# RWKV projections: both heads' keys written by two 128-partition VectorE operations, the second head's kinds change places in the store's DMAs

## The chip, the cores and the metric

The kernel runs on one core of one Trainium2 chip. The metric is the device time of one execution in microseconds (us), the median over several runs. Engine names are those of the profile: PE is the matrix engine, PEld its weight loads, DVE is VectorE, ACT is ScalarE, POOL is GpSimd and SP is SyncE, which issues almost every DMA of this kernel. A name with a q (SPq, DVEq) is an engine's instruction queue: DMA issues and waits.

## The reference

One block of a diffusion backbone, 512 latent tokens and 256 context tokens of width 1024, in two layers: the first mixes tokens with a bidirectional RWKV-7 recurrence, the second with a Hyena long convolution, each between two half-step SwiGLU layers. Only the RWKV mixer's preparation matters here. For each of 16 heads of 64 channels, two directions d and all 768 tokens it needs:

```
k   = xk @ w_k;  r = xr @ w_r;  v = xv @ w_v
a   = sigmoid(a0[d] + lora_a(xa)[d]);  decay = exp(-exp(-softplus(-w_pre[d]) - 0.5))
kk  = normalized(k * k_k)
kd  = k * (1 + (a - 1) * k_a)        # key of the direction
ka  = kk * a                         # removal key
S_t = S_{t-1} (diag(w_t) - kk_t ka_t^T) + v_t kd_t^T;   y_t = S_t r_t
```

The recurrence is computed in chunks of 64 tokens, so keys and queries are scaled with cumulated decays (`Ep`, `Em`) before they are used. The two scaled keys of a chunk, `ka * EK` and `kd * EK`, are the two kinds that this case is about.

## The kernel before, in words

All arithmetic is in f32; the large products split each operand in a high and a low part and take three matmuls (lines 471 to 473). Channels lie on the 128 partitions, tokens along the free dimension. A tile of 128 channels holds two heads: head 0 on partitions 0 to 63, head 1 on 64 to 127.

`rwkv_proj` (line 688) computes the projections one after the other: k, then r (line 901), v (line 910) and the gate's 160 columns (line 933). While r, v and the gate are projected, it draws steps out of `rwkv_prep` (line 943) with `ahead` (line 894), so that the preparation of the recurrence runs beside the matmuls. The order within an engine is worked out at compile time, by a scheduler that simulates the program; it takes what is issued first as the more urgent.

`rwkv_prep` works on 16 items: 8 tiles of 128 channels, each in two halves of 384 tokens (6 chunks of 64). Each item goes through three generators that run one pass apart: `front` loads k and r back from scratch memory (lines 975, 976), computes `kk` (line 982) from a small product on PE (line 980) and the low-rank products (lines 993, 994, 996, 997); `middle` makes the scaled keys and queries for both directions; `back` sums a bonus term (lines 1059 to 1066).

In `middle`, for each direction: line 1016 writes `ka` (one buffer), line 1019 is the scan over the decays, lines 1023 and 1024 are the two exponentials on ACT (`Ep` has one buffer), line 1021 writes `kd`, lines 1033 and 1034 write the tile `AR`, line 1036 the product `rb`. Lines 1039 to 1043 write the tile `KD`, of shape 128 x 6 chunks x 2 kinds x 64 tokens, with two buffers: head 0 holds (ka, kd) in the places 0 and 1, head 1 holds them the other way round, (kd, ka). So each of the two heads takes one operation for `ka` (line 1042) and one for `kd` (line 1043), 64 partitions each. Line 1042 is on POOL for the first 14 items and on DVE for the last two (line 1012, `NVEC` is 2); line 1043 is always on DVE. Then two DMAs on SP's queue store `AR` (line 1047) and `KD` (line 1050) into the scratch tensors `S_A` and `S_K`; a store of `KD` writes runs of 512 bytes, both kinds of one chunk side by side.

POOL has other work in the same stretch: line 1036 for the first 14 items, low parts of weights and of mixed tokens (line 477), low parts of the low-rank weights (line 963) and small memsets.

After the preparation `rwkv_scan` (line 1084) reads `S_A` and `S_K`: lines 1130 and 1134 load both kinds of two chunks, line 1198 is its first product, line 1152 loads one chunk of keys. They rely on the swapped places of head 1.

Stores whose shape bears on the change stand in line 926: they write v from 64 partitions in 6 runs of 256 bytes each, 96 KB in all.

Of the kernel before, what the change touches and what calls it, by code (L numbers as in the profile page):

```python
# [13 lines left out]
ALU = mybir.AluOpType  # L14
# [259 lines left out]
class K:  # L274
# [668 lines left out]
    def rwkv_prep(self, bp):  # L943
        nc = self.nc
        cE = 0.5 * math.exp(-0.5)
        W = TA // 2
        nch = W // 64
        c3 = lambda ap: ap.rearrange("p (c t) -> p c t", t=64)
        l2 = {}

        def ps(w):
            return self.psq.tile([P, 512], F32, tag="pq", name=self.nm("pq"))[:, :w]

        def T(tag, w=W, bufs=2):
            return bp.tile([P, W], F32, tag=tag, name=self.nm(tag), bufs=bufs)[:, :w]

        def lora2(m):
            raw = bp.tile([P, 4, P], F32, tag="l2r", name=self.nm("l2r"), bufs=1)
            hi = bp.tile([P, 4, P], F32R, tag="l2h", name=self.nm("l2h"), bufs=1)
            lo = bp.tile([P, 4, P], F32R, tag="l2l", name=self.nm("l2l"), bufs=1)  # L960
            nc.sync.dma_start(raw, self.A["wa2"][m])
            nc.scalar.copy(hi, raw)
            nc.gpsimd.tensor_tensor(lo, raw, hi.bitcast(F32), ALU.subtract)
            l2[m] = (hi, lo)

        lora2(0)

        def front(s):
            m, half = s["m"], s["half"]
            mc = slice(m, m + 1)  # L970
            o = s["o"] = half * W
            wl = s["wl"] = min(TL - o, W)
            s["nl"] = wl // 64
            k, r = T("k"), T("r", wl)
            nc.sync.dma_start(k, self.S_k[m][:, o : o + W])
            nc.sync.dma_start(r, self.S_r[m][:, o : o + wl])
            hi, lo = l2[m]
            yield
            pb = ps(W)
            nc.tensor.matmul(pb, self.selT[:, m * P : (m + 1) * P], self.kinv[:, o : o + W], start=True, stop=True)  # L980
            kk = s["kk"] = T("kk")
            nc.vector.scalar_tensor_tensor(kk, k, self.hkk[:, mc], pb, ALU.mult, ALU.mult)
            s["k"], s["r"] = k, r
            yield
            s["q"], s["a"] = [], []
            for d in range(2):
                q = bp.tile([P, nch, 65], F32, tag=f"q{d}", name=self.nm("q"))
                a = T(f"a{d}")
                nc.gpsimd.memset(q[:, :, 0:1], 0.0)
                rows = slice(d * 64, d * 64 + 64)  # L990
                for j, (x, t) in enumerate(((self.midw, q[:, :, 1:]), (self.mida, a))):
                    pt = ps(W)
                    nc.tensor.matmul(pt, hi[:, 2 * j + d], x[d][:, o : o + W], start=True, stop=False)
                    nc.tensor.matmul(pt, lo[rows, 2 * j + d], x[d][rows, o : o + W], start=False, stop=True)
                    b = (self.hw0, self.ha0)[j][:, d, mc]
                    nc.scalar.activation(t, c3(pt) if j == 0 else pt, AF.Tanh, bias=b, scale=0.5)
                nc.vector.tensor_scalar(q[:, :, 1:], q[:, :, 1:], 1.0, None, ALU.add)
                s["q"].append(q)
                s["a"].append(a)
                if d == 1 and half == 0 and m < DT - 1:  # L1000
                    lora2(m + 1)
                yield

        def middle(s):
            m, half, wl, nl = s["m"], s["half"], s["wl"], s["nl"]
            g, p_ = divmod(m, NP)
            c0 = s["o"] // 64
            mc = slice(m, m + 1)
            k, r, kk = s["k"], s["r"], s["kk"]
            s["b"] = []  # L1010

            pool = nc.vector if s["i"] >= 16 - NVEC else nc.gpsimd
            for d in range(2):
                q, a = s["q"][d], s["a"][d]
                ka, kd = T("ka", W, 1), a
                nc.vector.scalar_tensor_tensor(ka, a, 1.0, kk, ALU.add, ALU.mult)
                nc.scalar.activation(a, a, AF.Identity, bias=self.omka[:, mc], scale=self.hka[:, mc])
                qf = q.rearrange("p c t -> p (c t)")
                nc.vector.tensor_tensor_scan(qf, self.c("scan"), qf, 0.0, ALU.mult, ALU.add)
                yield  # L1020
                nc.vector.tensor_mul(kd, k, a)
                Ep = bp.tile([P, nch, 65], F32, tag="Ep", name=self.nm("Ep"), bufs=1)
                nc.scalar.activation(Ep, q, AF.Exp, scale=cE)
                nc.scalar.activation(q, q, AF.Exp, scale=-cE)
                Em = q
                nc.scalar.copy(self.PC[:, m, d, c0 : c0 + nch].unsqueeze(2), Em[:, :, 64:65])
                yield
                if d == 0:
                    EA, ER, EK = Em[:, :, 0:64], Em[:, :nl, 1:65], Ep[:, :, 1:65]
                else:  # L1030
                    EA, ER, EK = Ep[:, :, 1:65], Ep[:, :nl, 0:64], Em[:, :, 0:64]
                AR = bp.tile([P, nch, 2, 64], F32, tag="AR", name=self.nm("AR"), bufs=2)
                nc.vector.scalar_tensor_tensor(AR[:, :, 0], c3(kk), 2.0, EA, ALU.mult, ALU.mult)
                nc.vector.tensor_mul(AR[:, :nl, 1], c3(r), ER)
                rb = T("rb", wl, 1) if d == 0 else r
                pool.tensor_tensor(rb, r, kd[:, :wl], ALU.mult)
                s["b"].append(rb)
                yield
                KD = bp.tile([P, nch, 2, 64], F32, tag="KD", name=self.nm("KD"), bufs=2)
                for hh in range(2):  # L1040
                    h_ = slice(hh * 64, hh * 64 + 64)
                    pool.tensor_tensor(KD[h_, :, hh], c3(ka)[h_], EK[h_], ALU.mult)
                    nc.vector.tensor_mul(KD[h_, :, 1 - hh], c3(kd)[h_], EK[h_])
                if nl < nch:
                    nc.gpsimd.memset(AR[:, nl:, 1], 0.0)
                x = (g, d, half)
                nc.sync.dma_start(
                    self.S_A[x][:, :, p_].rearrange("c p s t -> p c (s t)"), AR.rearrange("p c s t -> p c (s t)")
                )
                nc.sync.dma_start(  # L1050
                    self.S_K[x][:, :, p_].rearrange("c p s t -> p c (s t)"), KD.rearrange("p c s t -> p c (s t)")
                )
                yield

        def back(s):
            m, wl, o = s["m"], s["wl"], s["o"]
            pt = ps(wl)
            rks = bp.tile([P, P], F32, tag="rks", name=self.nm("rks"), bufs=1)
            nc.scalar.activation(rks, self.c("bo64"), AF.Copy, scale=self.rk32[:, m : m + 1])
            yield  # L1060
            for d in range(2):
                nc.tensor.matmul(pt, rks, s["b"][d], start=d == 0, stop=d == 1)
            yield
            v = s["b"][0]
            nc.scalar.copy(v, pt)
            nc.sync.dma_start(self.S_b[s["m"]][:, o : o + wl], v)
            yield

        items = [dict(i=2 * m + 1 - half, m=m, half=half) for m in range(DT) for half in (1, 0)]
        n = len(items)  # L1070
        for i in range(n + 2):
            gens = []
            if 0 <= i - 2:
                gens.append(back(items[i - 2]))
            if 0 <= i - 1 < n:
                gens.append(middle(items[i - 1]))
            if i < n:
                gens.append(front(items[i]))
            while gens:
                gens = [x for x in gens if next(x, 0) is None]  # L1080
                yield
# [1031 lines left out]
```

## Time and profile before

| | us |
|---|---|
| median of 3 runs (lowest to highest) | 3119.48 (3110.41 to 3122.94) |
| the profiled execution's own time | 3117.68 |
| its span, first to last instruction | 3116.0 |
| PE busy in the span | 2848.1 (91%) |
| DVE busy | 1859.3 (60%) |
| ACT busy | 1202.1 (39%) |
| POOL busy | 504.5 (16%) |

The busy shares are averages over the whole kernel; the stretch in which `rwkv_prep` runs, from about 790 to 1050 us, looks otherwise. A row of a view of groups of instructions reads: line, engine, operation, tile written <- tiles read, shape, count, then busy us and mean ns of one, then the idle time of the engine just before them and what ended it. A row of windows reads: stretch, its length, busy us of each engine with the number of instructions, then the granted share of the TensorE clock, the mean busy share of the 16 DMA engines and the GB/s they moved.

### The profile page before, as it was taken

The page shows a single profiled execution, that of the slowest core. Times are in us where ns is not written, and L with a number is a line of the kernel's source. Part 1 is how long each engine was busy: PE and PEld are TensorE (multiplying, and loading weights), DVE is VectorE, ACT ScalarE, POOL GpSimd, SP SyncE. Part 2 cuts the span into 40 slices and gives each one's busy share as a digit, 9 for nine tenths or more (in the row PEclk, how much of TensorE's full clock was granted, in tenths as well). Part 3 has the DMA queues.
Part 4 walks back from the last instruction along what each step waited for, and adds up shares of the span by engine and source line. Part 5 has one row for each costly group of instructions (what it writes and reads, how often), then busy time and mean ns, then how long its engine had stood idle before and what let it go on. Part 6 is the DMA issues. An engine that isn't in the chain of part 4 may idle for free.

```text
span 3116.0 us, 46929 instructions
## 1 busy us (share of the span) xinstructions
PE 2848.1 (91%) x18698; PEld 2378.4 (76%) x18698; DVE 1859.3 (60%) x3261; ACT 1202.1 (39%) x2003; POOL 504.5 (16%) x571
## 2 busy tenths in 40 slices
PE   8999999978989567888799999999999988899998
PEld 4888888856656356776688889888896777888888
DVE  5744543473899778888754454554446578653334
ACT  3221121364555678885332222422234322242222
POOL 0000000032566344552100000000000044200000
PEclk9999999988979668898899999999999999999999
DMA  6533531313566643433634464344342454333221
GB/s 233 170 108 102 163 104 65 98 41 103 170 180 182 176 123 111 129 109 90 192 119 149 135 202 136 103 168 142 115 144 91 169 179 166 112 99 105 95 97 53
DMA packets 350084, 407.29 MB, mean 131 GB/s; under 512 B 52055, under 2 KB 289751, under 8 KB 348136
## 3 DMA queue, kind: packets, MB, share of 16 engines
q1 hardware_dynamic: 349864, 404.29, 40.9%
q8 instruction: 147, 2.41, 0.3%
q14 instruction: 73, 0.60, 0.1%
HBM read 338.10 MB, written 65.34 MB: 129 GB/s over the span
## 4 chain that ended last, share of the span: by engine, by line
PE 49%; DVE 7%; ACT 5%; DMA 2%; issue 2%; POOL 1%; SPq 0%; DVEq 0%; POOLq 0%; ACTq 0%
PE ps L471 14%; PE ps L472 14%; PE ps L473 14%; PE sc L1198 1%; ACT XT L1288 1%; ACT AG L1174 1%; DVE Dl L1265 1%; DVE wlo L477 1%; DVE Tm L1258 1%; PE pf L1747 1%; ACT Dl L1223 1%; DVE zl L477 1%; DVE SV L1337 1%; DVE zt L1934 1%; PE ps L414 0%
## 5 line engine op out<-in xcount | busy, mean ns | idle before, releaser
L471 PE MATMUL ps<-hh,whi 128*128 128x512 f32 (+1 forms) x2064 | 733.3, 363 | 14.3 <-ACT hh L264 11.0
L472 PE MATMUL ps<-hl,whi 128*128 128x512 f32 (+1 forms) x2064 | 742.6, 362 | 3.0 <-DVE hl L265 3.0
L473 PE MATMUL ps<-hh,wlo 128*128 128x512 f32 (+1 forms) x2064 | 736.5, 362 | 1.6 <-DVE wlo L477 1.6
L477 DVE TENSOR_TENSOR wlo<-raw,whi 128x1024 fp32r<-128x1024 f32 (+1 forms) x325 | 392.4, 1213 | 407.0 <-ACT whi L476 402.9
L476 ACT CAST whi<-raw 128x1024 fp32r<-128x1024 f32 (+1 forms) x338 | 344.5, 1028 | 720.0 <-PE ps L472 648.7
L471 PEld LDWEIGHTS ps<-hh,whi 128*128 128x128 f32 x2064 | 386.6, 190 | 79.7 <-ACT hh L264 13.3
L472 PEld LDWEIGHTS ps<-hl,whi 128*128 128x128 f32 x2064 | 393.0, 190 | 62.8 <-DVE hl L265 4.0
L473 PEld LDWEIGHTS ps<-hh,wlo 128*128 128x128 f32 x2064 | 391.9, 190 | 64.2 <-DVE wlo L477 2.3
L472 PE MATMUL ps<-dl,whi 128*128 128x512 f32 (+1 forms) x1072 | 358.1, 335 | 0.0
L473 PE MATMUL ps<-dh,wlo 128*128 128x512 f32 (+1 forms) x1072 | 357.8, 335 | 0.0
L471 PE MATMUL ps<-dh,whi 128*128 128x512 f32 (+1 forms) x1072 | 356.8, 337 | 0.0
L601 DVE TENSOR_TENSOR sg<-sg,ps 128x512 f32<-128x512 f32 (+1 forms) x110 | 69.1, 632 | 259.1 <-PE ps L473 249.7
L472 PEld LDWEIGHTS ps<-dl,whi 128*128 128x128 f32 x1072 | 204.2, 191 | 20.4
L471 PEld LDWEIGHTS ps<-dh,whi 128*128 128x128 f32 x1072 | 203.8, 191 | 20.9
L473 PEld LDWEIGHTS ps<-dh,wlo 128*128 128x128 f32 x1072 | 203.9, 190 | 20.6
L408 DVE SCALAR_TENSOR_TENSOR macc<-mraw,cs,macc 128x1024 f32<-128x1024 f32 x133 | 168.7, 1282 | 81.7 <-DMA mraw<-in_mod_w 80.5
L1779 POOL TENSOR_SCALAR G<-G 128x512 f32<-128x512 f32 x8 | 11.9, 1492 | 937.3 <-ACT G L1770 919.9
L600 ACT ACTIVATE sg<-ps 128x512 f32<-128x512 f32 (+1 forms) x110 | 59.6, 552 | 229.8 <-PE ps L473 216.9
L476 ACT CAST dh<-sg 128x512 fp32r<-128x512 f32 (+1 forms) x110 | 62.4, 575 | 214.0 <-DVE sg L601 213.8
L472 PE MATMUL ps<-xl,whi 128*128 128x512 f32 (+2 forms) x336 | 131.3, 392 | 11.0 <-DVE xl L798 6.3
L471 PE MATMUL ps<-xh,whi 128*128 128x512 f32 (+2 forms) x336 | 128.3, 395 | 10.2 <-ACT xh L805 6.5
L647 DVE SCALAR_TENSOR_TENSOR x<-ps,der,x 128x512 f32<-128x512 f32 (+1 forms) x128 | 82.5, 663 | 84.4 <-PE ps L473 84.3
(315 smaller groups left out, 4759.5 us busy)
## 6 DMA issues: line engine op xcount, KB each, us to landing
raw<-in_wgu SPq DMA_DIRECT2D x88, 1024.0 KB, 5.0
mraw<-in_mod_w SPq DMA_DIRECT2D x144, 512.0 KB, 4.3
raw<-in_wd SPq DMA_DIRECT2D x24, 1024.0 KB, 4.8
raw<-in_wrkv SPq DMA_DIRECT2D x12, 1024.0 KB, 5.2
S_A<-AR SPq DMA_DIRECT2D x32, 384.0 KB, 3.2
S_K<-KD SPq DMA_DIRECT2D x32, 384.0 KB, 3.3
AG<-S_A SPq DMA_DIRECT2D x48, 256.0 KB, 4.2
KK<-S_K SPq DMA_DIRECT2D x24, 512.0 KB, 4.5
```

What stands on the lines that cost most here:

```text
L408: nc.vector.scalar_tensor_tensor(acc, raw, sc, acc, ALU.mult, ALU.add)
L471: nc.tensor.matmul(out, wh, xh, start=start, stop=False)
L472: nc.tensor.matmul(out, wh, xl, start=False, stop=False)
L473: nc.tensor.matmul(out, wl, xh, start=False, stop=stop)
L476: self.nc.scalar.copy(hi, src)
L477: (self.nc.gpsimd if pool else self.nc.vector).tensor_tensor(lo, src, hi.bitcast(F32), ALU.subtract)
L600: nc.scalar.activation(sg, pg, AF.Silu)
L601: nc.vector.tensor_mul(sg, sg, pu)
L647: nc.vector.scalar_tensor_tensor(X[m][:, o : o + w], pt, gates[who][:, m : m + 1], X[m][:, o : o + w], ALU.mult, ALU.add)
L1174: nc.scalar.copy(dst, src)
L1198: nc.tensor.matmul(sc[:, p_, :, :ns, :], KK[:, c, p_].rearrange("p s t -> p (s t)"), AG[:, c, :, p_, :ns, :], start=True, stop=True,)
L1223: nc.scalar.copy(BD[r].rearrange("p t c -> p c t"), Bcc[r, :, b : b + 32])
```

## The change

The two kinds of both heads are written to the same places, so that one operation of 128 partitions writes `ka` for both heads and one writes `kd`; both are on DVE, for all 16 items. The places of head 1 are swapped in the store: where one DMA stored `KD`, three do, one for head 0 (64 partitions, runs of 512 bytes) and one for each kind of head 1 (64 partitions, runs of 256 bytes, 96 KB each). What lies in `S_K` is the same as before.

```
                 KD = bp.tile([P, nch, 2, 64], F32, tag="KD", name=self.nm("KD"), bufs=2)
-                for hh in range(2):
-                    h_ = slice(hh * 64, hh * 64 + 64)
-                    pool.tensor_tensor(KD[h_, :, hh], c3(ka)[h_], EK[h_], ALU.mult)
-                    nc.vector.tensor_mul(KD[h_, :, 1 - hh], c3(kd)[h_], EK[h_])
+                nc.vector.tensor_mul(KD[:, :, 0], c3(ka), EK)
+                nc.vector.tensor_mul(KD[:, :, 1], c3(kd), EK)
                 if nl < nch:
                     nc.gpsimd.memset(AR[:, nl:, 1], 0.0)
                 x = (g, d, half)
                 nc.sync.dma_start(
                     self.S_A[x][:, :, p_].rearrange("c p s t -> p c (s t)"), AR.rearrange("p c s t -> p c (s t)")
                 )
-                nc.sync.dma_start(
-                    self.S_K[x][:, :, p_].rearrange("c p s t -> p c (s t)"), KD.rearrange("p c s t -> p c (s t)")
-                )
+
+                sk = self.S_K[x][:, :, p_].rearrange("c p s t -> p c s t")
+                nc.sync.dma_start(sk[:64].rearrange("p c s t -> p c (s t)"), KD[:64].rearrange("p c s t -> p c (s t)"))
+                for j in range(2):
+                    nc.sync.dma_start(sk[64:, :, 1 - j], KD[64:, :, j])
                 yield
```

## Rows read from the trace of the kernel before

**Rows 1.** Windows: busy us of each engine, granted clock, DMA share, GB/s.

```profile
790.00:820.00 30.00, 30.00 (x121) 21.45 (x121) 28.27 (x35) 20.22 (x39) 16.48 (x18) 1.00 0.66 195
790.00:1022.00 232.00, 200.03 (x785) 139.74 (x785) 221.32 (x274) 136.31 (x281) 145.70 (x146) 0.85 0.65 184
1022.00:1050.00 28.00, 15.29 (x45) 7.38 (x43) 26.88 (x49) 16.76 (x32) 5.64 (x6) 0.74 0.57 158
```

**Rows 2.** Groups of instructions by shape, DVE, 790 to 1022 us.

```profile
L1019 DVE TENSOR_TENSOR_SCAN q<-cst,q 128x390 f32<-128x390 f32 x29 | 39.6, 1366 | 0.9
L1021 DVE TENSOR_TENSOR a<-k,a 128x384 f32<-128x384 f32 x28 | 26.1, 931 | 1.8 <-ACT a L1017 1.8
L1043 DVE TENSOR_TENSOR KD<-a,q 64x384 f32<-64x384 f32 x28 | 25.1, 898 | 0.7
L1016 DVE SCALAR_TENSOR_TENSOR ka<-a,kk 128x384 f32<-128x384 f32 x29 | 25.0, 864 | 1.6 <-ACT a L996 1.3
L1043 DVE TENSOR_TENSOR KD<-a,Ep 64x384 f32<-64x384 f32 x28 | 23.7, 847 | 1.6 <-ACT Ep L1023 1.3
L997 DVE TENSOR_SCALAR q<-q 128x384 f32<-128x384 f32 x29 | 16.2, 559 | 1.4 <-ACT q L996 1.0
L1033 DVE SCALAR_TENSOR_TENSOR AR<-kk,q 128x384 f32<-128x384 f32 x14 | 11.6, 827 | 2.5 <-ACT q L1024 2.3
L1033 DVE SCALAR_TENSOR_TENSOR AR<-kk,Ep 128x384 f32<-128x384 f32 x14 | 10.4, 741 | 0.1
```

**Rows 3.** The same view, DVE, 1026 to 1050 us, where POOL is nearly idle.

```profile
L1019 DVE TENSOR_TENSOR_SCAN q<-cst,q 128x390 f32<-128x390 f32 x3 | 2.9, 963 | 0.0
...
L1043 DVE TENSOR_TENSOR KD<-a,Ep 64x384 f32<-64x384 f32 x4 | 2.2, 550 | 0.0
...
L1033 DVE SCALAR_TENSOR_TENSOR AR<-kk,Ep 128x384 f32<-128x384 f32 x2 | 1.1, 550 | 0.0
...
L997 DVE TENSOR_SCALAR q<-q 128x384 f32<-128x384 f32 x2 | 0.7, 343 | 0.0
```

**Rows 4.** The same view, POOL, 790 to 1022 us.

```profile
L1042 POOL TENSOR_TENSOR KD<-ka,q 64x384 f32<-64x384 f32 x28 | 34.1, 1219 | 23.2 <-ACT q L1024 16.1 <-DVE ka L1016 4.5 <-DVE AR L1034 1.5
L1042 POOL TENSOR_TENSOR KD<-ka,Ep 64x384 f32<-64x384 f32 x28 | 33.1, 1183 | 16.7 <-ACT Ep L1023 11.4 <-ACT PC L1026 3.1 <-issue 0.6
```

**Rows 5.** Waits of PE, 790 to 1022 us: total us, times, longest.

```profile
PE ps L919 <- ACT ev L828: 7.3, 6, 3.8
PE ps L471 <- ACT xh L476: 3.7, 2, 2.7
```

**Rows 6.** Timeline of DVE, last item: start us, us, line, operation.

```profile
1047.65 0.54 DVE L1042 TENSOR_TENSOR KD<-ka,q 64x384 f32<-64x384 f32 x1
1048.12 0.54 DVE L1043 TENSOR_TENSOR KD<-a,q 64x384 f32<-64x384 f32 x1
1048.68 0.56 DVE L1042 TENSOR_TENSOR KD<-ka,q 64x384 f32<-64x384 f32 x1
1049.16 0.55 DVE L1043 TENSOR_TENSOR KD<-a,q 64x384 f32<-64x384 f32 x1
1049.74 0.56 DVE L1036 TENSOR_TENSOR r<-r,a 128x384 f32<-128x384 f32 x1
```

**Rows 7.** Lines 1050 and 926: issue of a store, ns min/median/max, first and last start.

```profile
L1050 SPq DMA_DIRECT2D S_K<-KD x32: 359/371/2082, 799.0 to 1049.7; - x32
...
L926 SPq DMA_DIRECT2D S_V<-vt x32: 587/632/2837, 892.5 to 1015.1; - x32
```

**Rows 8.** DMA issues, 790 to 1050 us: count, KB each, median us to landing.

```profile
S_K<-KD SPq DMA_DIRECT2D x32, 384.0 KB, 3.3
...
S_V<-vt SPq DMA_DIRECT2D x32, 96.0 KB, 2.5
```

**Rows 9.** Timeline of SP and PE where the scan begins.

```profile
1046.17 0.54 SPq L1050 DMA_DIRECT2D S_K<-KD  x1
1046.76 0.62 SPq L1134 DMA_DIRECT2D KK<-S_K  x1
...
1050.99 3.76 PE L1198 MATMUL ps<-AG,KK 128*128 128x128 f32 x16 [4.86 <-issue]
```

## The prediction

> **What bounds the kernel now.** I read the page first: PE is 91% busy over the span, DVE 60%, POOL 16%. These averages say nothing about the place that the change touches, so the windows over the stretch of the preparation come next [rows 1]. From 790 to 1022 us DVE is busy 221.3 of 232 us, 95%, and in the tail to 1050 us 26.9 of 28, 96%. PE is busy 200.0 of the 232 us, at a mean granted clock of 0.85 of its upper level, 2.4 GHz. So DVE sets the pace here, and PE, whose matmuls stand in order between the preparation's small products, waits for what DVE makes. Only in the first 30 us is PE full, at clock 1.00.
>
> The second reading is what DVE's busy time is made of: the same operation compared in two stretches. From 1026 us on POOL has almost nothing left, and a DVE operation on 384 elements with two inputs takes 550 ns, the scan 963, line 997 343 [rows 3]. Before 1022 us, with POOL at work, the same shapes take 741 to 931, 1366 and 559 ns [rows 2]. The extra time is no work; it is what a neighbour costs. Over the eight groups of rows 2 it is 28 x 381 + 28 x 348 + 28 x 297 + 29 x 314 + 14 x 277 + 14 x 191 for the operations of 384 elements, 29 x 403 for the scan and 29 x 216 for line 997: 62.4 us.
>
> **What the change removes.** First, 56 operations of line 1042 leave POOL, 34.1 + 33.1 = 67.2 us [rows 4] of the 145.7 us that POOL is busy in the stretch [rows 1], 46%. If each us of POOL costs DVE alike, 0.46 x 62.4 = 28.8 us of DVE's extra time go with them. The bounds: nothing, if the remaining POOL work (lines 477, 963, 1036) meets DVE all the more; and 62.4 us, if only these operations were to blame. I take 28.8, since rows 2 show the extra time in all eight groups and so no reason to blame one POOL line more than another.
>
> Secondly, the operations on one head. Two that start on the same head follow each other in 0.47 or 0.48 us, while a change of head takes 0.56 to 0.58 [rows 6]. For the first 28 direction passes DVE does two operations before and two after, of the same 384 elements per partition, so 128 partitions cost no more than 64; but the two changes of head go, 2 x 0.09 x 28 = 5.0 us. In the last four passes line 1042 is on DVE itself: four operations, 2.09 us from the first to what follows, become two of 0.47, so 4 x 1.15 = 4.6 us.
>
> **What becomes time.** In the 232 us DVE would need 28.8 + 5.0 = 33.8 us less. PE has 32.0 us of idle time there [rows 1], of which 7.3 us wait for ACT's copies of v and 3.7 for ACT's high parts [rows 5]; these need not shorten. So at the clock it had, PE could give up 21.0 us; were it granted the upper level throughout, its 200.0 us would be 170 and DVE the only limit. I take the middle of 21.0 and 33.8: 27.4 us. The tail's 4.6 us count in full, since DVE is the busy engine there and no POOL work covers it.
>
> **What it adds.** 64 DMA issues on SP's queue: 32 stores of 384 KB become 32 of 192 KB and 64 of 96 KB. The near row is line 926: its stores have the very shape of the new ones, 64 partitions in runs of 256 bytes, and take 632 ns to issue and 2.5 us to land, against 371 ns and 3.3 us for a store of `KD` now [rows 7, 8]. So an issue costs between 0.37 and 0.63 us, 24 to 40 us of SP's time in all, beside 260 us in which SP mostly waits for tiles; I cost it at nothing there. What would uncover it is a load of k or r queued behind the stores: the one DVE waits for is line 982's k, an item ahead. `KD` itself comes free only when three stores have landed instead of one; its two buffers give it a whole direction pass, 260 / 32 = 8.1 us, and the new landing is at most 1.3 us of issues later than now, so that costs nothing either unless the passes halve.
>
> At the end the queue does show. The scan's second load of keys is issued right behind a store of `KD`, and PE's first product starts at 1050.99 us, 3.6 us after that issue ended [rows 9]. Two stores of the last two items stand ahead of it, four more issues: 1.5 to 2.5 us. I take 2.0.
>
> **The sum:** -27.4 - 4.6 + 2.0 = -30.0 us, from the profiled execution's 3117.7 to 3087.7. The median shown is 1.8 us above that execution, so the forecast for the median is 3089.5 us, 1.0% less. By the bounds: DVE's whole 33.8 us with 4.6 and an exposed 1.5 give 3082.6; nothing from POOL (5.0 + 4.6 - 2.5) gives 3112.4.
>
> **The rivals.** A measurement of this kernel can tell about 0.5%, 15.6 us, from no change.
>
> *Faster than that.* POOL's key operations may do more harm than their share. If they were to blame for all of the extra time, DVE would need 62.4 + 5.0 us less and PE would be the limit: 170 us at the upper level plus the 11 us of waits on ACT, 181 instead of 232. Then -51 - 4.6 + 2 gives about 3066. Against it: the groups are slowed alike, and PE would have to get the full clock, where it had 0.85. The Trainium skill, page SBUF — State Buffer, section Who interferes with whom, has VectorE operations with two inputs and GpSimd operations that read SBUF exclude each other for a whole instruction. By that rule up to all 67.2 us of line 1042 could have held DVE, which would speak for this rival; rows 2 and 4, by shares, give 28.8. Chance 0.08.
>
> *PE takes over at once.* If PE's waits in the stretch come from its own order and from ACT rather than from DVE, and its clock stays, only some 5 us of the 232 can go: -5 - 4.6 + 2, 3112. For it: PE is 86% busy there, and full in the first 30 us. Against it: DVE's idle time is 5%. Chance 0.10.
>
> *POOL's other work takes the lock's place.* The 78 us of POOL work that stay meet DVE as often as all 146 did: the 5.0 + 4.6 - 2.0 us that hang on no such meeting remain, 3112. It needs POOL to have been waiting rather than DVE. Chance 0.09.
>
> *Slower: the stores hold up the loads.* SP issues in order. Per item, four more issues of 0.63 us and a landing of 2.5 us stand ahead of the next k: 5.0 us. It decides from the point where k lands later than DVE's turn at line 982; with no margin left DVE would idle 16 x 5.0 = 80 us, and with the 38.4 us gained in work the time would be 3161. For it: the v projection's bursts of four stores already load the queue. Against it: in none of the groups of rows 2 does a DMA end DVE's idle time, and the loads run an item ahead. The Trainium skill, DMA: Bandwidth & Descriptors, section Specifications, speaks against the change here: below 512 bytes a transfer is not at line rate and becomes a read-modify-write. The trace has such runs in line 926, and they land in 2.5 us. If the 32 x 192 KB were moved twice, an estimate by that page, it would be 6.3 MB at 184 GB/s, 34 us, beside DMA engines idle for 35% of 232 us. Chance 0.09, with whatever else a new order of the instructions may spoil.
>
> That the change doesn't do what it says is no case: the diff takes line 1042 off POOL in plain sight.
>
> **How the numbers follow.** Forecast 0.64, the larger gain 0.08, PE 0.10, POOL 0.09, slower 0.09. The forecast and the larger gain are faster by over 0.5% (under 3103.9): 0.72. PE and POOL's other work are within 0.5%: 0.19. Slower 0.09. The range runs from 3070, which takes in the forecast with some clock given back to PE and leaves out the whole of the larger gain, to 3116, past both cases at 3112; it leaves out 0.17 and the edges of the forecast.
>
> **What would show it.** Right: no line 1042 on POOL; the scan's mean near 1.17 us instead of 1.37 and the 384-element groups near 0.70; the stretch to the last `KD` about 30 us shorter, with DVE still over 90% busy; S_K issues near 0.5 us. Wrong: DVE's groups at 0.8 us and more as before; DVE below 85% with PE full, or with idle time that a DMA or k ends; a start of the scan more than 3 us after the last key load.

## The result, and the profile after

The changed kernel takes **3080.45 us** (median of 4 runs, 3075.51 to 3085.6) against 3119.19 us of the kernel before measured beside it: a ratio of 0.9879, 95% interval 0.9858 to 0.9899, so 1.2% less. A second measurement, told below, gave 0.9863. The forecast was 3089.5 us, the range 3070 to 3116; direction and range held, the gain was 9 us larger than forecast.

The account starts from the page. Head of the page and busy times, kernel after (engine, busy us, share of the span, instructions):

```profile
span 3073.7 us, 46929 instructions
PE 2822.9 (92%) x18698; PEld 2362.3 (77%) x18698; DVE 1811.0 (59%) x3253; ACT 1203.1 (39%) x2003; POOL 434.7 (14%) x515
```

The span is 42.3 us shorter (3116.0 before). PE is busy 25.2 us less (2848.1 before) and idle 17.1 us less. The 18698 products are the same, so the 25.2 us read as time that the same matmuls took at a lower clock; the windows below bear that out. DVE is busy 48.3 us less (1859.3), and POOL 69.8 us less (504.5). Of DVE's 48.3, by the prediction's own prices 5.0 are changes of head and 4.6 the last passes; the other 38.7 us are operations that became shorter.

Windows to the end of the gate product, the last large product beside the preparation, first before, then after (columns as in [rows 1]):

```profile
790.00:1035.00 245.00, 212.83 (x825) 146.11 (x824) 234.21 (x295) 143.97 (x298) 149.90 (x150) 0.85 0.64 180
```

```profile
790.00:988.00 198.00, 185.90 (x811) 131.65 (x811) 184.80 (x280) 139.04 (x286) 81.10 (x92) 0.96 0.85 216
```

The same large products end 47 us earlier (14 of the preparation's small ones are left for later: 811 against 825). PE's idle time fell from 32.2 to 12.1 us, and its busy time by 26.9 us while the granted clock rose from 0.85 to 0.96; 212.83 x 0.85 / 0.96 is 188, near the 185.9 that PE took. DVE is still busy 93% of the stretch, but PE is now busy 94% of it: the two limits lie together. DVE's busy time in the stretch fell by 49.4 us, with 15 operations fewer in it: the 47 us seen from DVE and from PE are the same time, and are not to be added.

Groups of instructions by shape, DVE, 790 to 990 us, after, beside [rows 2]:

```profile
L1019 DVE TENSOR_TENSOR_SCAN q<-cst,q 128x390 f32<-128x390 f32 x30 | 33.3, 1109 | 1.2
L1016 DVE SCALAR_TENSOR_TENSOR ka<-a,kk 128x384 f32<-128x384 f32 x29 | 21.5, 743 | 0.8 <-ACT a L996 0.5
L1021 DVE TENSOR_TENSOR a<-k,a 128x384 f32<-128x384 f32 x28 | 18.5, 665 | 1.8 <-ACT a L1017 1.5
L997 DVE TENSOR_SCALAR q<-q 128x384 f32<-128x384 f32 x30 | 16.5, 549 | 4.2 <-ACT q L996 4.2
L1041 DVE TENSOR_TENSOR KD<-a,Ep 128x384 f32<-128x384 f32 x14 | 12.9, 918 | 0.0
L1040 DVE TENSOR_TENSOR KD<-ka,Ep 128x384 f32<-128x384 f32 x15 | 10.7, 713 | 2.7 <-ACT Ep L1023 1.3 <-DMA S_K<-KD 1.2
L1041 DVE TENSOR_TENSOR KD<-a,q 128x384 f32<-128x384 f32 x14 | 9.5, 677 | 0.1
...
L1040 DVE TENSOR_TENSOR KD<-ka,q 128x384 f32<-128x384 f32 x14 | 8.8, 627 | 0.0
L1033 DVE SCALAR_TENSOR_TENSOR AR<-kk,q 128x384 f32<-128x384 f32 x14 | 8.7, 624 | 1.3 <-ACT a L996 1.3
L1033 DVE SCALAR_TENSOR_TENSOR AR<-kk,Ep 128x384 f32<-128x384 f32 x14 | 8.5, 610 | 0.1
```

The scan's mean fell from 1366 to 1109 ns, line 1021's from 931 to 665. The new writes of `KD` (lines 1040 and 1041) take 627 to 918 ns for 128 partitions, against 847 and 898 for 64 before. At the quiet prices of [rows 3] the eight groups of rows 2 (line 1041 standing for 1043) now carry 28.2 us of extra time instead of 62.4, and line 1040 another 3.5: 31.7, or 30.7 less.

The stores, lines 1050 (head 0) and 1052 (the kinds of head 1), issue in ns and landing in us, after, beside [rows 7, 8]:

```profile
L1050 SPq DMA_DIRECT2D S_K<-KD x32: 574/587/986, 796.3 to 1017.2; - x32
...
DMA to landing us min/median/max: 2.9/3.4/5.9
```

```profile
L1052 SPq DMA_DIRECT2D S_K<-KD x64: 574/623/2027, 795.6 to 1017.8; - x64
...
  DVE KD L1040: 1.2, 2
...
DMA to landing us min/median/max: 2.3/3.2/7.3
```

The middle row of the second fence is who waited for them: DVE's next writes of `KD`, 1.2 us in all, twice.

### The profile page after: what moved, and what is told of

It is laid out like the page before. It is cut to its first block, busy times and chain, and to the rows that moved or that the text cites. A ratio compares the mean times of both kernels' runs of the same rounds, so it can differ in the third digit from the quotient of the medians.

```text
span 3073.7 us, 46929 instructions
## 1 busy us (share of the span) xinstructions
PE 2822.9 (92%) x18698; PEld 2362.3 (77%) x18698; DVE 1811.0 (59%) x3253; ACT 1203.1 (39%) x2003; POOL 434.7 (14%) x515
## 2 busy tenths in 40 slices
DMA packets 363394, 407.28 MB, mean 133 GB/s; under 512 B 77655, under 2 KB 303063, under 8 KB 361448
## 4 chain that ended last, share of the span: by engine, by line
PE 75%; DVE 11%; ACT 6%; DMA 4%; issue 3%; POOL 1%; SPq 0%; DVEq 0%; ACTq 0%; POOLq 0%
PE ps L471 21%; PE ps L473 21%; PE ps L472 21%; PE sc L1198 1%; PE ps L414 1%; ACT Dl L1223 1%; DVE wlo L477 1%; ACT XT L1288 1%; DVE Dl L1265 1%; ACT AG L1174 1%; DVE xm L743 1%; DVE Tm L1258 1%; PE pf L1747 1%; DVE SV L1337 1%; DVE zt L1934 1%
## 5 line engine op out<-in xcount | busy, mean ns | idle before, releaser
L476 ACT CAST dh<-sg 128x512 fp32r<-128x512 f32 (+1 forms) x110 | 62.4, 576 | 213.5 <-DVE sg L601 213.4
L1779 POOL TENSOR_SCALAR G<-G 128x512 f32<-128x512 f32 x8 | 11.9, 1492 | 938.2 <-ACT G L1770 920.5
L472 PE MATMUL ps<-xl,whi 128*128 128x512 f32 (+2 forms) x336 | 124.8, 373 | 11.5 <-DVE xl L798 6.7
L471 PE MATMUL ps<-xh,whi 128*128 128x512 f32 (+1 forms) x336 | 120.9, 372 | 9.8 <-ACT xh L805 6.5
```

Source lines behind the costliest of these rows:

```text
L471: nc.tensor.matmul(out, wh, xh, start=start, stop=False)
L472: nc.tensor.matmul(out, wh, xl, start=False, stop=False)
L476: self.nc.scalar.copy(hi, src)
```

## The experiments

Ratios are to the kernel before, run on the same chip beside each; 0.001 is 3.1 us. The theory: POOL's 56 operations held DVE up for about half of their own length, and taking them away let both DVE and, through it, PE go faster. Rivals: POOL's remaining operations take their place; `ka` and `Ep`, which POOL kept occupied, were what DVE waited for; the merging of the heads did it, not POOL; the stores cost what limits the gain.

**1. The POOL operations put back, on other data.** In the changed kernel POOL gets 56 extra operations of 64 partitions that read only `kk` and write a tile nobody reads.

```
                 nc.vector.tensor_mul(KD[:, :, 1], c3(kd), EK)
+                if pool is nc.gpsimd:
+                    for hh in range(2):
+                        h_ = slice(hh * 64, hh * 64 + 64)
+                        Z = bp.tile([P, 5, 64], F32, tag="Z", name=self.nm("Z"), bufs=1)
+                        nc.gpsimd.tensor_tensor(Z[h_], c3(kk)[h_, :5], c3(kk)[h_, :5], ALU.mult)
```

> The changed kernel, with 56 operations put back on POOL (two per direction pass of the first 14 items, 64 partitions x 320 elements, 5/6 of line 1042's old size) that multiply kk with itself into a tile that nobody reads. VectorE's work, the stores and every result that another engine waits for stay those of the changed kernel. Theory (POOL's operations hold up VectorE's while they run): VectorE's groups are stretched again, and 5/6 of the 34 us that the trace of before shows on VectorE's instructions beside line 1042 come back, 20 to 29 us: 3100 to 3110 us. Rival (the gain came from results of POOL that others waited for, or from the stores' new order): nothing waits for these operations, so 3077 to 3085 us, and VectorE's groups keep the means of the changed kernel.

Measured: 3108.74 us, 0.9966 (0.9955 to 0.9978): 28 us of the gain are gone. Groups by shape, POOL and DVE, 790 to 1022 us, this kernel:

```profile
L1046 POOL TENSOR_TENSOR Z<-kk 64x320 f32<-64x320 f32 x56 | 58.5, 1045 | 14.2 <-DVE kk L982 11.0
```

```profile
L1019 DVE TENSOR_TENSOR_SCAN q<-cst,q 128x390 f32<-128x390 f32 x32 | 40.1, 1255 | 1.3
...
L997 DVE TENSOR_SCALAR q<-q 128x384 f32<-128x384 f32 x32 | 21.0, 658 | 2.5 <-ACT q L996 2.4
...
L1040 DVE TENSOR_TENSOR KD<-ka,Ep 128x384 f32<-128x384 f32 x15 | 15.2, 1017 | 0.6 <-ACT Ep L1023 0.3
L1040 DVE TENSOR_TENSOR KD<-ka,q 128x384 f32<-128x384 f32 x15 | 13.4, 891 | 0.9 <-ACT q L1024 0.8
```

DVE's own operations became longer again, and DVE never waits for the new tile. Over the whole program DVE is busy 1834.1 us, 23.1 more than after, with the same operations: 0.39 us for each us that these POOL operations take. POOL's mere presence, with nobody waiting for these operations, costs DVE that time. A part of the 28 us can have come another way: POOL's own results (line 1036) come later behind the new operations, and PE waits 7.9 us for them from 790 to 1022 us, 2.1 in after.

**2. The same operations, on `ka` and the decays.** As 1, but POOL reads `c3(ka)[h_, :5]` and `EK[h_, :5]`, so that DVE and ACT also wait for it before they rewrite these tiles.

> The changed kernel with POOL's operations of line 1042 put back as they were read, ka times the decays, 64 partitions x 320 elements, into a tile that nobody reads. Beside what the operations on kk cost (3109 us), ka and the decays now stay occupied until POOL has read them, as in the kernel before. Theory: the hold-up of VectorE's instructions is most of it, 0 to 6 us more than with kk, 3105 to 3115 us. Rival that the buffers held back were worth as much: over 3118 us.

Measured: 3116.91 us, 0.9978 (0.9969 to 0.9988), just above what was expected and below the rival. DVE is busy 1844.7 us, 33.7 more than after and 10.6 more than in run 1. By medians this is 8 us above run 1, by ratios, which are to their own runs of before, 4 us with overlapping intervals. Held tiles are thus worth 4 to 8 us at most, and whether they cost anything beside the hold-ups stays unsettled. DVE waits for the new operations once in this trace, 1.5 us.

**3. Off POOL, but not merged.** In the kernel before, line 1042 runs on DVE for all items, and the store is one DMA as before.

```
                     h_ = slice(hh * 64, hh * 64 + 64)
-                    pool.tensor_tensor(KD[h_, :, hh], c3(ka)[h_], EK[h_], ALU.mult)
+                    nc.vector.tensor_mul(KD[h_, :, hh], c3(ka)[h_], EK[h_])
                     nc.vector.tensor_mul(KD[h_, :, 1 - hh], c3(kd)[h_], EK[h_])
```

> The kernel before with line 1042 on VectorE for all items: four operations on half the partitions per direction pass, and the one store of before. Theory: VectorE gets 56 operations more at 0.55 us, 31 us, and is rid of 34 us of waiting for POOL: about the time of before, 3108 to 3122 us. Rival that merging the partitions is what counts and POOL's part is free: VectorE is the limit and pays the 31 us, 3140 to 3150 us. Rival that POOL's late results were what others waited for: they are gone, 3080 to 3095 us.

Measured: 3108.56 us, 0.9969 (0.9958 to 0.9979). The half of the change that takes work off POOL gives about 10 us by itself. DVE is busy 1852.1 us, only 7.2 less than before: the 56 operations that it took over are 56 x 0.55 (the quiet price of [rows 3]) = 30.8 us, so what became shorter is worth 38.0 us. By the spacing of starts in [rows 6] the price is lower: the four operations of a pass take 2.09 us, two with a change of head about 1.14, so 28 x 0.95 = 26.6 us, and what became shorter is 33.8 us. So the 38.7 us found above come out here, by another way, as 34 to 38.

**4. Merged, but `ka` on POOL.** In the changed kernel the `ka` operation of 128 partitions goes to POOL for the first 14 items.

```
-                nc.vector.tensor_mul(KD[:, :, 0], c3(ka), EK)
+                pool.tensor_tensor(KD[:, :, 0], c3(ka), EK, ALU.mult)
```

> The changed kernel with the one operation of ka for both heads on POOL for the first 14 items (28 operations of 128 partitions x 384). Theory: VectorE gives up 28 x 0.47 = 13 us and waits 28 x 0.6 = 17 us for POOL, half of what line 1042's 56 operations cost before: 3 to 8 us slower than the changed kernel, 3080 to 3090 us; so partitions that are computed for nothing are what the half operations cost, on POOL as on VectorE. Rival that POOL's share is work taken off VectorE: 3062 to 3072 us.

Measured: 3085.8 us, 0.9876 (0.9855 to 0.9897), not to be told from the changed kernel. POOL's groups, 790 to 1022 us, beside [rows 4]:

```profile
L1040 POOL TENSOR_TENSOR KD<-ka,q 128x384 f32<-128x384 f32 x14 | 16.2, 1154 | 19.2 <-ACT q L1024 14.9 <-DVE ka L1016 2.2 <-ACT rks L1059 2.0
L1040 POOL TENSOR_TENSOR KD<-ka,Ep 128x384 f32<-128x384 f32 x14 | 15.8, 1129 | 12.7 <-ACT Ep L1023 8.4 <-DVE ka L1016 4.2
```

On POOL, too, 128 partitions take no longer than 64 (1183 and 1219 ns before), so merging alone halves what it does there, 67.2 to 32.0 us, and halves DVE's own writes as well. Runs 3 and 4 together divide the change: moving alone gives about 10 us, merging alone, with its stores, about 36; together they would make more than the whole change, so part of the gain can be had either way. Once merged, where `ka` runs hardly matters: DVE saves 28 operations and pays for them in hold-ups (busy 1816.8 against 1811.0 us). PE, to the end of the gate product in this run:

```profile
790.00:998.00 208.00, 195.57 (x815) 137.08 (x815) 188.61 (x254) 138.19 (x286) 105.78 (x120) 0.90 0.80 204
```

Its idle time, 12.4 us, is that of after, but it was granted 0.90 and took 9.7 us longer over nearly the same products.

**5. No reading POOL operation left.** In the changed kernel every POOL operation that reads a tile goes to DVE from r's projection on: `rb`, the low parts of line 477 and of line 963.

```
+            self.wpool = False
             prep = self.rwkv_prep(bp)
...
-                    self.split(a, b, t, m % MXP == 1)
+                    self.split(a, b, t, self.wpool and m % MXP == 1)
...
-            nc.gpsimd.tensor_tensor(lo, raw, hi.bitcast(F32), ALU.subtract)
+            nc.vector.tensor_tensor(lo, raw, hi.bitcast(F32), ALU.subtract)
...
-                pool.tensor_tensor(rb, r, kd[:, :wl], ALU.mult)
+                nc.vector.tensor_mul(rb, r, kd[:, :wl])
```

> The changed kernel with POOL's remaining operations that read tiles moved to VectorE from the r projection on: line 1036 (28), line 963 and POOL's share of line 477; POOL keeps its memsets. Theory: the 41 us that VectorE's instructions still lose beside these operations vanish, and VectorE gains some 30 us of work (28 products of 0.2 to 0.5 us, 8 low parts of 1.2, 8 of 0.7 to 0.95, 7 of 0.7): 3062 to 3078 us, with the scan's mean at 0.97 us. Rival that POOL's operations run beside VectorE for nothing: 30 us more, 3100 to 3112 us.

Measured: 3075.12 us, 0.9862 (0.9848 to 0.9877). Groups, DVE, 790 to 985 us, and the window (lines from 891 on stand one further down):

```profile
L1020 DVE TENSOR_TENSOR_SCAN q<-cst,q 128x390 f32<-128x390 f32 x31 | 29.7, 961 | 0.2
...
L998 DVE TENSOR_SCALAR q<-q 128x384 f32<-128x384 f32 x31 | 11.3, 365 | 0.8 <-ACT q L997 0.8
...
L1041 DVE TENSOR_TENSOR KD<-ka,Ep 128x384 f32<-128x384 f32 x15 | 8.2, 550 | 1.3 <-ACT Ep L1024 1.3
```

```profile
790.00:985.00 195.00, 187.59 (x818) 131.70 (x816) 173.69 (x335) 140.77 (x290) 7.99 (x42) 0.96 0.84 217
```

These operations are within 22 ns of their quiet prices in [rows 3], in the middle of the stretch, with the DMA engines as busy as after. So the extra time of [rows 2] came from POOL's reading operations, and none of it that can be seen from PE, ACT or the DMAs. Yet the kernel is not faster than after by anything that can be told: DVE is down to 89% of the stretch and PE up at 96%, clock 0.96 as after. This reads as PE's own work being the limit from here on; no run tested that.

**6 and 7. `rb` alone moved to DVE, twice.** As the last edit of run 5, alone.

> The changed kernel with line 1036 on VectorE for all items, POOL's other operations left. Theory: 12 us of waiting vanish, 28 products of 0.47 and 0.2 us (9 us) are added: 3074 to 3081 us. Rival that POOL's products run beside VectorE for nothing: 9 us more, 3088 to 3092 us.

Measured: 3075.02 us, 0.9845 (0.9828 to 0.9861). This looked like a version that beats the changed kernel, so it was run again, beside the changed kernel:

> Line 1036 on VectorE as well, as in the run that gave 3075 us. Theory (12 us of waiting for POOL against 9 us of work): 2 to 7 us faster than the changed kernel beside it, 3073 to 3079 us. Rival that PE and its clock are now the limit and the earlier difference was chance: the same as the changed kernel within 2 us.

> The changed kernel itself, beside the next two on one chip, so that they can be told apart: 3076 to 3086 us by both theories.

Measured: 3077.69 us, 0.9866 (0.985 to 0.9883), against the changed kernel's 3075.09 us, 0.9863 (0.9846 to 0.9881). The advantage did not come back. No version was found that beats the changed kernel.

**8. The store in three, in the kernel before.** One DMA for head 0 and two for head 1, with no kinds swapped; the added lines, which replace the one store:

```
+                sk = self.S_K[x][:, :, p_].rearrange("c p s t -> p c s t")
+                nc.sync.dma_start(sk[:64].rearrange("p c s t -> p c (s t)"), KD[:64].rearrange("p c s t -> p c (s t)"))
+                for j in range(2):
+                    nc.sync.dma_start(sk[64:, :, j], KD[64:, :, j])
```

> The kernel before, its store of KD cut into the three DMAs of the changed kernel, without the swap: the change's DMA side alone. Doubling the swapped stores of the changed kernel gave 9 us where 0 to 5 were expected. If the stores cost about the same at first, 3 to 12 us more than the kernel before, 3121 to 3131 us; if they are covered where VectorE sets the pace, 0 to 3 us more, 3118 to 3122 us.

Measured: 3125.61 us, 1.0014 (1.0005 to 1.0024): 4 us slower. The prediction costed the stores at 2.0 us in all, at the end; here they cost 4, in a kernel that has none of the gain. What they cost within the changed kernel no run shows.

**9. The swapped stores twice.** In the changed kernel each kind of head 1 is stored two times, 64 more DMAs.

```
-                for j in range(2):
+                for j in (0, 0, 1, 1):
                     nc.sync.dma_start(sk[64:, :, 1 - j], KD[64:, :, j])
```

> The changed kernel with each of the two swapped stores of head 1 issued twice (64 DMA issues more on SP, 6 MB more written, the same bytes). Theory that the stores are covered: 0 to 5 us more, 3080 to 3086 us. Rival that the stores already cost part of the gain (SP's queue, runs of 256 bytes): 64 issues of 0.6 us show, 15 to 40 us more, 3095 to 3120 us.

Measured: 3089.48 us, 0.9909 (0.9894 to 0.9924), 9 us above the first measurement of the changed kernel and 14 above the second, between the two expectations. Waits of DVE, 790 to 1040 us (us in total, times, longest):

```profile
DVE KD L1040 <- DMA S_K<-KD: 14.1, 8, 6.0
DVE kk L982 <- DMA k<-S_k: 5.5, 4, 2.3
```

What gives first is not the load of k, the slower rival's place, but `KD`'s two buffers, which wait for the last of their stores to land; the load is second. After has the first wait with 1.2 us [the row above] and the second not at all, so the changed kernel stands near the edge: with 64 issues more, DVE waits 19.6 us for these two where it waited 1.2.

**10. DVE's end lengthened.** For the last item the changed kernel writes `KD` nine times over, 32 more operations of 0.47 us each, 15 us, all after the gate product.

```
+                if s["i"] == 15:
+                    for _ in range(8):
+                        nc.vector.tensor_mul(KD[:, :, 0], c3(ka), EK)
+                        nc.vector.tensor_mul(KD[:, :, 1], c3(kd), EK)
```

> The changed kernel with the two operations that write KD repeated eight times more in both directions of the last item alone (32 operations of 0.47 us, 15 us of VectorE at the very end of the preparation, behind the gate's product). If the preparation's tail on VectorE sets when the scan begins, as the prediction had it, 13 to 17 us more: 3093 to 3098 us. If the gate's product sets it and the tail runs beside the scan's beginning, 0 to 6 us more: 3080 to 3086 us, with the scan's first product as early as in the changed kernel.

Measured: 3086.83 us, 0.9898 (0.9877 to 0.9919), 11.7 us above the changed kernel in the same series (the two intervals just touch) and 6.4 above its first measurement. Times in us, read from the timelines; "gate" is the start of line 936, the first step after the gate's product:

| | gate | last `KD` ends | scan's first product | span |
|---|---|---|---|---|
| before | 1037.4 | 1049.7 | 1051.0 | 3116.0 |
| after | 989.7 | 1015.5 | 1004.6 | 3073.7 |
| run 10 | 986.0 | 1028.1 | 1000.5 | 3084.4 |
| run 9 | 996.4 | 1035.0 | 1024.6 | 3092.5 |
| run 5 | 985.4 | 999.9 | 1001.7 | 3072.8 |
| after, measured again | 998.2 | 1023.4 | 1012.5 | 3076.2 |

The scan's first product comes 13.6 us after the gate before, 14.9 and 14.2 after, 14.5 in run 10 and 16.3 in run 5, and 12 to 18 in the other runs; in run 10 it came 28 us before the last `KD` was written. (In run 9 it took 28.2, and PE's weight loads waited 5.0 us for a store of `KD` there.) So the last key does not open the scan; that the end of the projections does is read from this spacing, and no run tested it. But the padding was paid for all the same, later: waits of DVE, run 10, 1015 to 1110 us.

```profile
DVE Tm L1249 <- DMA S_K<-KD: 3.7, 1, 3.7
```

A step of the scan (line 1245 in the changed kernel) waits there for the store of the padded keys. That is 3.7 of the 11.7 us; where the rest went was not looked into. Nor does the table say which mark sets the end of the span. From the last `KD` to the end it is 2052.8 to 2075.9 us over all the traces, from the scan's first product 2063.7 to 2083.9, and the two traces of the changed kernel itself differ by 5.4 us in either: its second trace came to the scan 7.9 us later and ended 2.5 us later. What a microsecond at the end of the preparation is worth is therefore not settled closer than that.

## Why the prediction was right, and where it was off

**What bounds the stretch: right.** DVE set the pace (busy 95% of it), and part of its busy time was POOL's doing. Run 5 shows it in full: with no POOL reads, DVE's groups stand at the prices of [rows 3].

**The price of POOL's operations: right, but counted over too few groups.** The prediction took "If each us of POOL costs DVE alike, ... 28.8 us". Over the groups that it looked at, 30.7 went. Over all of DVE's operations it was 38.7 in the change and 34 to 38 in run 3: groups outside rows 2 became shorter too, some 8 us that the sum had left out, 4.5 of them line 1034 (18.0 to 13.5 us over its shapes). POOL's remaining 81.8 us to 990 leave 31.7 us of extra time in these groups and line 1040, 0.39 for each us, where it was 62.4 / 145.7 = 0.43 before; the rival in which POOL's other work takes the lock's place falls. The rule of the Trainium skill, SBUF — State Buffer, section Who interferes with whom, that such operations exclude each other for a whole instruction, agrees in kind with run 1, where POOL operations that DVE never waits for made DVE's own longer. The prediction's upper end by that rule, all 67.2 us, was not reached: 38.7 / 67.2 is 0.58.

**What becomes time: the term that was mis-sized.** The prediction put the stretch at -27.4 us, between PE's idle time at the old clock (21.0) and DVE's relief (33.8). The two do not bound it: the gate product came 47 us earlier. PE gave up 20.1 us of idle time, as the first figure has it, and 26.9 us of its busy time besides, at a granted clock of 0.96 instead of 0.85. The prediction named this clock (200.0 us would be 170 at the upper level), but took from it only half of the way to DVE's relief, and had that relief too small, 33.8 us against 43.7 (38.7 and 5.0). That the clock rises when PE's gaps close is not a fixed price: run 4 has the same idle time at 0.90.

The last `KD`, DVE's own end, came 34.2 us earlier, near the 32.0 that the terms give for it (27.4 + 4.6). That nearness is luck: the gate gained 20 us more than its term, and the way from the gate to the last `KD` became 13.5 us longer, 25.8 instead of 12.3, where the prediction had it 4.6 shorter. Window behind the gate, after:

```profile
990.00:1016.00 26.00, 13.04 (x47) 9.17 (x46) 14.51 (x32) 19.46 (x42) 4.06 (x9) 0.63 0.92 247
```

DVE is busy 56% of it, not the 96% of [rows 1] on which the 4.6 us rested: more of the preparation is left when the gate ends (33 operations of DVE up to the last `KD`, 23 before), and of the 11.5 us that DVE is idle 10.2 end with a result of ACT.

**The end: the wrong chain, in part.** The prediction let DVE's tail open the scan, and costed two stores' issues ahead of the second load of keys at +2.0. Timelines of SP and PE, after: the stores ahead of the first two loads of keys, these loads, and the last stores; then the scan's first product.

```profile
994.30 0.64 SPq L1050 DMA_DIRECT2D S_K<-KD  x1
994.99 0.95 SPq L1052 DMA_DIRECT2D S_K<-KD  x1
...
997.98 0.59 SPq L1134 DMA_DIRECT2D KK<-S_K  x1
998.66 1.23 SPq L1130 DMA_DIRECT2D AG<-S_A  x2
999.99 0.54 SPq L1134 DMA_DIRECT2D KK<-S_K  x1
...
1016.48 0.60 SPq L1052 DMA_DIRECT2D S_K<-KD  x1
1017.17 0.59 SPq L1050 DMA_DIRECT2D S_K<-KD  x1
1017.82 0.64 SPq L1052 DMA_DIRECT2D S_K<-KD  x1
```

```profile
1004.58 3.75 PE L1198 MATMUL ps<-AG,KK 128*128 128x128 f32 x16 [7.47 <-ACT a L1017]
```

The product starts 12 us before the last stores are issued, so the stores of the last item do not stand ahead of it. Stores of an earlier pass do, in a row of issues without a break up to the second load; whether they cost a part of the 2.0 us no run shows. The product starts 4.0 us after the issue of that load ended, 3.6 before: by its letter, "more than 3 us after the last key load", a sign of being wrong, but one that the kernel before shows as well. The gate came 47.7 us earlier, the scan's first product 46.4, the last `KD` 34.2, and the span is 42.3 shorter. The tail's 4.6 us could not be seen by themselves; run 10 shows that DVE's time there counts for something in the changed kernel, 6 to 12 of 15 us.

**The stores: costed too low.** SP's issues take 32 x 0.587 + 64 x 0.623 = 58.7 us instead of 32 x 0.371 = 11.9, so 46.8 us more, where 24 to 40 were given: the 64 new issues cost 39.9 of that, and the store of head 0, half a tile, costs 0.216 us more than that of the whole tile did, which the prediction left out. Run 8 puts the cost in time at 4 us; the slower rival's 80 us of idle DVE did not come. That the release of `KD` by three landings costs nothing was right to 1.2 us, and wrong as soon as the stores grew (run 9).

**The rivals.** "PE takes over" was wrong about when: PE had 47 us to give, not 5, and by run 5, which gains nothing more, may have taken over after that. The larger gain of 3066 us erred to the right side: more hold-up, and most of the clock given back (0.96); it would have needed all 62.4 us. Of the signs named, the scan's mean came to 1.11 us (1.17 forecast), the groups of 384 elements to 0.61 to 0.92 (0.70), DVE's share to 93% (over 90%), an S_K issue to 0.6 us (0.5).

**What carries the gain.** The prediction ascribed nearly all of it to POOL. Runs 3 and 4 show that this needs the merging: 56 more half-height operations on DVE cost 27 to 31 of the 34 to 38 us that leaving POOL freed.

## What to carry to other kernels

Before work is moved from one engine to another, see whether two operations on half the partitions can be one: on DVE and on POOL alike 128 partitions took the time of 64, and the swapped order that stood in the way could be left to the DMAs for some 4 us. Compare the same operation in a stretch where the neighbour engine works and in one where it rests, over all of an engine's groups; the difference, here 0.4 to 0.6 us of DVE for each us of POOL, is time that no list of waits shows. And when the engine that starves PE is relieved, reckon with PE's busy time at the higher granted clock too: here it fell by 26.9 us at 0.96, more than PE's gaps did (20.1); run 4, with the same gaps at 0.90, shows that the higher clock is not sure to come.

## What the runs showed that was not expected

A store of half the partitions took longer to issue, not shorter: 371 ns for 128 partitions and 384 KB, 587 ns for 64 partitions in runs of 512 bytes, 623 ns for 64 partitions in runs of 256 bytes; in run 8 the last two took 586 and 587 ns, so the runs are not what makes it dear. The last two landed in 3.4 and 3.2 us, in run 8 in 3.0 and 2.7. The shorter runs carry half the bytes (96 against 192 KB), so these times show no large price for them, but cannot exclude a small one; the page counts 77655 packets under 512 bytes after, 25600 more than before. The mechanism behind the dearer issue of 64 partitions was not looked into.

A POOL operation on 128 x 384 elements took 1.13 to 1.15 us, one on 64 x 384 1.18 to 1.22 [rows 4], and one on 64 x 320 1.05 (run 1), all of them beside a DVE at work.
